# A hybrid attention block: VectorE's order written out in more places, results added to the output by stores, sums of weight chunks taken one chunk sooner in the last stage

## The chip, the core and the metric

The kernel runs on one core of one Trainium2 chip. The metric is the device time of one execution in microseconds. Three timed executions of the kernel before gave 2165.52, 2166.34 and 2167.77 us; the median is 2166.34. A profiled execution, taken separately, is where all durations come from.

## What is computed

One residual block over 512 tokens of width 2048, in float32:

```
h    = rms_norm(x) ; proj = h @ w_in          # 15424 columns, split into branches and gates
conv = (B * conv3(C * u)) * silu(conv_z) @ w_conv_out            # 1024 channels
mla  = attention(16 heads, low-rank q and kv, rotary keys, block-causal) * silu(mla_z) @ w_mla_out
memo = attention(4 heads of 256 over 256 memory tokens) * silu(mem_z) @ w_mem_out
merged = sigmoid(g1) * conv + sigmoid(g2) * mla + sigmoid(g3) * memo
out  = x + merged @ w_o
```

## The kernel before

**Products in three parts.** Each float32 operand is split into a high part, which ScalarE rounds to TensorE's reduced float32 (`act.activation(hi, src, Copy)`), and a low part, which VectorE subtracts (`lo = src - hi`). A product is three matmuls: high by high, high by low, low by high (`mm3`, L161 to L163). So every weight needs one ScalarE and one VectorE instruction before TensorE can use all of it.

**Panels.** The three large projections (w_h, the regrouped columns of w_in, then w_mla_out and w_o) use a scheme with seven products in place of eight for each 2x2 block of blocks. A panel is 256 output columns and takes four chunks of weights; per chunk TensorE makes 42 matmuls of 256 columns. `pair_weights` handles one chunk in three stages: load 512 KB into a `raw` tile (four buffers, L274); three VectorE sums of quarters into the same tile (L276 to L278); the split, `whi` by ScalarE (L281) and `wlo` by VectorE (L282), two buffers each. At a panel's end VectorE adds the four PSUM banks up into an `e` tile (L318 to L327, after a ScalarE copy at L317). The operand on the other side, `xp` or `xo`, is treated alike once for each of eight pairs: `pair_sums` (L255 to L258), then `pair_split` (L261, L262).

**The queue of chunks.** All weight chunks, of panels and of plain groups, stand in one list. `take` is called once for each chunk that TensorE is about to use: it brings this chunk and the next to the split, the one after to its sums, the fourth to its load, then runs one entry of `fills`, a list of postponed pieces of other work, and returns the chunk. Eight first chunks of a projection are ordered (0,0) (0,1) (0,2) (1,0) (1,1) (1,2) (0,3) (1,3) as (panel, chunk), so that pairs 6 and 7 of x can come late and two panels end one right after the other.

**Stages, in time.** Memory keys and values (four groups of eight chunks); x is normalised and split beside it; 60 w_h panels, whose results `finish` sends on (for the first eight panels the sums of squares and both parts, `keep_sums` and `keep_parts`); attention heads interleaved with their projections; the conv projection interleaved with memory attention (`mem_attend`, in the order `ORDER_MEM`: digits step a head, w steps the conv projection); w_mla_out; the memory projection in five groups, the last of four small chunks, beside which the merged results are loaded and turned into `xo`; w_o in eight panels, and the result. A step table, `steps_out`, says after which chunk of the memory projection each piece of merged work is done.

**Order on the engines.** TensorE's and SyncE's orders are those of the program text throughout. VectorE's is that of the text only inside a `manual_schedule` context: from step 27 of the memory keys to six steps into w_h, and from the memory projection to nine steps into w_o. Elsewhere a scheduler orders VectorE when the kernel is built, by its own estimate of times; it may also put an instruction from behind such a stretch between those of the stretch. ScalarE is always ordered by the scheduler. SyncE loads weights and most inputs; GpSimd issues loads and stores of scratch tensors, the accumulating stores into `mgdram` among them; ScalarE issues some stores.

**The result.** In each w_o panel but the last, `middle` (at the second chunk) loads the matching 512 KB of x into an `xr` tile (two buffers, L1341), and one chunk after the panel's end `result` adds `e` to it in two VectorE instructions (L1350) and stores the halves from ScalarE's queue (L1351). The last panel has a tail of its own, `tail_o`.

**Memory attention.** For each head two half steps of scores; each has a maximum (L1152), its scaled negative (L1155), two exponentials with their sums (L1159), a reciprocal (L1162) and two scalings of p (L1164). Then p is transposed by TensorE (L363), split, multiplied with the values, gated (L1180) and stored.

Of the kernel before, what the change touches and what calls it, by code (L numbers as in the profile page):

```python
# [20 lines left out]
F32 = mybir.dt.float32  # L21
# [86 lines left out]
def body(ctx, tc, a, out):  # L108
# [73 lines left out]

    def take(ahead=1):
        for at in range(1 + ahead):
            begin(at, 3)
        begin(1 + ahead, 2)
        begin(2 + ahead, 1)
        if fills:
            fills.pop(0)()
        return queue.pop(0)[4]  # L190
# [339 lines left out]
    work = panels(xp, a["w_h"], len(SEQUENCE), lambda n: make(n), lambda n, e: finish(n, e), "aux")  # L530
# [54 lines left out]
    begin(2, 2)  # L585
# [175 lines left out]

    def make(n):
        return etile(), None
# [57 lines left out]
    for _ in range(6):  # L821
        next(work)
# [15 lines left out]
    PLACES = ((2, 3), (6, 7), (4, 5), (0, 1))  # L838
# [292 lines left out]
    def mem_attend(head):  # L1131
# [11 lines left out]
        pr = []  # L1143
        for i2 in range(2):
# [16 lines left out]
            ri = pq.tile([P, 2], F32, tag="ri", name="ri", bufs=2)  # L1161
            vec.reciprocal(ri, sm)  # L1162
            for ii in range(2):
                act.activation(p[:, ii], p[:, ii], AF.Copy, scale=ri[:, ii:ii + 1])  # L1164
                pr.append(p[:, ii])
            yield
        pts = []
        for j in range(2):
            b = transpose4([t[:, j * P:(j + 1) * P] for t in pr])
# [19 lines left out]
    run(ORDER_MEM, w=conv, **{str(n): m[n] for n in range(4)})  # L1189
# [102 lines left out]
    def split_out(n):  # L1292
# [11 lines left out]
                 29: ((sums_out, 4),), 30: ((split_out, 4), (merged, 6)), 31: ((sums_out, 5),),  # L1304
                 32: ((split_out, 5),)}
# [9 lines left out]
    for tag, width in (("acc", 512), ("aux", 512), ("acc", 512), ("aux", 256), ("aux", 256)):  # L1315
        if done == 7:
            work = panels(xp, a["w_o"], 8, lambda n: make_o(n), lambda n, e: finish_o(n, e),
                          tail=lambda b, e: tail_o(b, e))
        banks = [bank(tag) for _ in range(width // P)]
# [18 lines left out]
    def make_o(n):  # L1338
        def middle():
            xrs[n] = pe.tile([P, 2, S], F32, tag="xr", name="xr", bufs=2)  # L1340
            nc.sync.dma_start(xrs[n].rearrange("p f n -> p (f n)"), a["xT"][:, n])  # L1341
        return pe.tile([P, 8, H], F32, tag="e", name="e", bufs=2), middle

    def finish_o(n, e):
        fills.append(lambda: result(n, e))

    def result(n, e):
        xr = xrs[n]
        for f in range(2):
            vec.tensor_tensor(out=xr[:, f], in0=two(e)[:, f], in1=xr[:, f], op=ALU.add)  # L1350
            nc.scalar.dma_start(out[(2 * n + f) * P:(2 * n + f + 1) * P], xr[:, f])  # L1351
# [16 lines left out]
    fills += [lambda: None, lambda: sums_out(6), lambda: split_out(6), lambda: sums_out(7), lambda: split_out(7)]  # L1368
# [82 lines left out]
```

## Time and profile before

| | us |
|---|---|
| median of three timed executions | 2166.34 |
| profiled execution, its own time | 2162.43 |
| span of its instructions | 2160.7 |
| TensorE busy | 2122.6 |
| VectorE busy | 1728.2 |
| ScalarE busy | 1010.8 |
| GpSimd busy | 130.9 |
| mean granted TensorE clock | 0.998 |

A line of a timeline has the start, the duration, the engine, the line of the program, the instruction, its output and inputs with shapes, and in brackets how long the engine sat idle before it and what ended that. A line of the view of waits has who waited for whom, the sum in us, how often, and the longest. Matmuls overlap, so their durations are longer than their spacing.

### The profile page before, as it was taken

How to read it: one execution, taken by the hardware profiler on the slowest of the kernel's cores; microseconds unless marked ns; L12 is line 12 of the kernel's file. 1: busy time of each engine (PE TensorE's matmuls, PEld its weight loads, DVE VectorE, ACT ScalarE, POOL GpSimd, SP SyncE). 2: the span in 40 equal slices, each digit the busy share in tenths (PEclk: the TensorE clock that was granted, in tenths of full speed). 3: DMA queues.
4: the chain of work that ended last, by engine and by line, in shares of the span. 5: the costliest groups of instructions: out<-in, count | busy, mean ns of one | idle time of the engine just before them, and what ended most of it. 6: DMA issues, size and time to landing. Idle time of an engine off the chain costs nothing.

```text
span 2160.7 us, 38707 instructions
## 1 busy us (share of the span) xinstructions
PE 2122.6 (98%) x16040; PEld 2037.7 (94%) x16040; DVE 1728.2 (80%) x2740; ACT 1010.8 (47%) x1235; POOL 130.9 (6%) x189
## 2 busy tenths in 40 slices
PE   9989999999999999999999999999999999999899
PEld 7889999999999999999999999898988899987899
DVE  5986878888888888888878876788886688856886
ACT  6743444444444344344444444777765533323333
POOL 0000000000000000000000000212111100011000
PEclk9999999999999999999999999999999999999999
DMA  8634443333333333343444336222346957667443
GB/s 330 248 98 137 158 135 128 128 127 128 127 127 127 125 125 126 126 136 133 137 137 142 131 129 241 90 104 81 112 158 245 355 203 208 201 213 199 141 162 107
DMA packets 93441, 338.51 MB, mean 157 GB/s; under 512 B 10896, under 2 KB 11152, under 8 KB 91216
## 3 DMA queue, kind: packets, MB, share of 16 engines
q1 hardware_dynamic: 70848, 252.58, 34.5%
q0 software_dynamic: 13920, 59.51, 8.6%
q10 hardware_dynamic: 8496, 23.94, 3.1%
q8 instruction: 125, 2.05, 0.4%
q14 instruction: 52, 0.43, 0.1%
HBM read 273.34 MB, written 62.65 MB: 156 GB/s over the span
## 4 chain that ended last, share of the span: by engine, by line
PE 84%; DVE 5%; ACT 2%; DMA 2%; issue 1%; POOL 0%; DVEq 0%; ACTq 0%; POOLq 0%
PE acc L161 14%; PE acc L163 14%; PE acc L162 14%; PE aux L161 13%; PE aux L163 13%; PE aux L162 13%; DVE wlo L282 2%; PE aux L363 1%; PE aux L997 1%; DMA raw<-in_w_h 1%; ACT whi L281 1%; DVE raw L276 0%; PE aux L977 0%; PE aux L980 0%; PE aux L978 0%
## 5 line engine op out<-in xcount | busy, mean ns | idle before, releaser
L281 ACT ACTIVATE whi<-raw 128x1792 fp32r<-128x1792 f32 x304 | 517.6, 1703 | 795.6 <-PE aux L162 336.7
L282 DVE TENSOR_TENSOR wlo<-raw,whi 128x1792 fp32r<-128x1792 f32 x304 | 614.8, 2022 | 204.2 <-ACT whi L281 203.5
L163 PE MATMUL aux<-xp,wlo 128*128 128x256 f32 (+1 forms) x1712 | 479.8, 280 | 6.3 <-DVE wlo L282 6.2
L161 PE MATMUL aux<-xp,whi 128*128 128x256 f32 (+1 forms) x1712 | 480.4, 281 | 0.0
L162 PE MATMUL aux<-xp,whi 128*128 128x256 f32 (+1 forms) x1712 | 479.2, 280 | 0.0
L163 PE MATMUL acc<-xp,wlo 128*128 128x256 f32 x1680 | 470.2, 280 | 3.4 <-DVE wlo L282 3.4
L161 PE MATMUL acc<-xp,whi 128*128 128x256 f32 x1680 | 470.8, 280 | 0.0
L162 PE MATMUL acc<-xp,whi 128*128 128x256 f32 x1680 | 469.6, 280 | 0.0
L163 PEld LDWEIGHTS aux<-xp,wlo 128*128 128x128 f32 (+1 forms) x1712 | 321.1, 188 | 7.5 <-DVE wlo L282 7.5
L161 PEld LDWEIGHTS aux<-xp,whi 128*128 128x128 f32 (+1 forms) x1712 | 320.6, 187 | 0.0
L163 PEld LDWEIGHTS acc<-xp,wlo 128*128 128x128 f32 x1680 | 316.0, 188 | 4.6 <-DVE wlo L282 4.6
L162 PEld LDWEIGHTS aux<-xp,whi 128*128 128x128 f32 (+1 forms) x1712 | 320.2, 187 | 0.0
L161 PEld LDWEIGHTS acc<-xp,whi 128*128 128x128 f32 x1680 | 315.6, 188 | 0.0
L162 PEld LDWEIGHTS acc<-xp,whi 128*128 128x128 f32 x1680 | 315.1, 188 | 0.0
L276 DVE TENSOR_TENSOR raw<-raw 128x512 f32<-128x512 f32 x304 | 208.3, 685 | 36.5 <-DMA raw<-in_w_h 31.8
L155 DVE TENSOR_TENSOR wlo<-raw,whi 128x1024 fp32r<-128x1024 f32 (+2 forms) x89 | 100.5, 1131 | 75.1 <-ACT whi L154 72.7
L154 ACT ACTIVATE whi<-raw 128x1024 fp32r<-128x1024 f32 (+2 forms) x89 | 87.7, 986 | 101.4 <-PE acc L162 43.3
L278 DVE TENSOR_TENSOR raw<-raw 128x256 f32<-128x256 f32 x304 | 127.9, 422 | 6.3
L277 DVE TENSOR_TENSOR raw<-raw 128x256 f32<-128x256 f32 x304 | 127.9, 422 | 5.7
L161 PE MATMUL acc<-whi,blk 128*128 128x384 f32 (+1 forms) x224 | 84.2, 376 | 0.0
L356 POOL TENSOR_TENSOR rs_r<-rs_t,mhalf 128x2 f32<-128x2 f32 (+2 forms) x71 | 65.2, 929 | 276.7 <-DVE rs_t L355 217.2
L163 PE MATMUL acc<-whi,blk 128*128 128x384 f32 (+1 forms) x224 | 80.9, 361 | 0.0
(360 smaller groups left out, 3896.7 us busy)
## 6 DMA issues: line engine op xcount, KB each, us to landing
raw<-in_w_h SPq DMA_DIRECT2D x240, 512.0 KB, 3.5
raw<-in_w_mla_out SPq DMA_DIRECT2D x32, 512.0 KB, 4.2
raw<-in_w_o SPq DMA_DIRECT2D x32, 512.0 KB, 3.6
raw<-in_w_mem_kv SPq DMA_DIRECT2D x31, 512.0 KB, 7.4
gdram<-e ACTq DMA_DIRECT2D x22, 512.0 KB, 2.9
raw<-in_w_ukv SPq DMA_DIRECT2D x16, 512.0 KB, 4.3
raw<-in_w_conv_out SPq DMA_DIRECT2D x16, 512.0 KB, 8.3
aadram<-z POOLq DMA_DIRECT2D x8, 896.0 KB, 3.9
```

The costliest lines, as they stand in the source:

```text
L154: act.activation(hi[:, cols], raw[:, cols], AF.Copy)
L155: vec.tensor_tensor(out=lo[:, cols], in0=raw[:, cols], in1=r32(hi[:, cols]), op=ALU.subtract)
L161: nc.tensor.matmul(o, lhsT=s[0], rhs=m[0], start=start, stop=False, skip_group_check=shared)
L162: nc.tensor.matmul(o, lhsT=s[0], rhs=m[1], start=False, stop=False, skip_group_check=shared)
L163: nc.tensor.matmul(o, lhsT=s[1], rhs=m[0], start=False, stop=stop, skip_group_check=shared)
L276: vec.tensor_tensor(out=f[:, 4:6], in0=f[:, 1:3], in1=f[:, 0:1].to_broadcast([P, 2, 256]), op=ALU.add)
L277: vec.tensor_tensor(out=f[:, 6], in0=f[:, 5], in1=f[:, 1], op=ALU.add)
L278: vec.tensor_tensor(out=f[:, 7], in0=f[:, 6], in1=f[:, 3], op=ALU.add)
L281: act.activation(hi, f[:, 1:8], AF.Copy)
L282: vec.tensor_tensor(out=lo, in0=f[:, 1:8], in1=r32(hi), op=ALU.subtract)
L356: pool.tensor_tensor(out=r, in0=t, in1=mhalf[:, :n], op=ALU.pow)
L363: nc.tensor.transpose(out=b[:, i * P:(i + 1) * P], in_=s, identity=ident)
```

## The change

Ten edits, in the order of the program:

- `take` gets a list `deeper`; for each entry in it the sums and the load reach one chunk further. An entry is put in ahead of the last group of the memory projection, so from there on sums are done for the third and fourth chunk, and the load for the fifth.
- `finish` of the first two w_h panels is postponed by way of `fills`.
- Ahead of w_h, its third chunk is only loaded (`begin(2, 1)`), not summed.
- In w_h panels 12 to 18, SyncE copies x, 512 KB a panel, from its input in DRAM straight to the output in DRAM.
- VectorE's written order in w_h ends after nine steps, not six.
- The places in memory of two pairs of latent blocks are exchanged (`PLACES`).
- In `mem_attend` the reciprocal and scalings of the first half step follow the exponentials of the second, and those of the second stand ahead of the first transposes.
- The run over `ORDER_MEM` gets a written VectorE order.
- The split of pair 5 of the merged results moves from the end of the memory projection to the first w_o chunk (to `fills`, where the empty entry was).
- The results of the first seven w_o panels are added to the output by accumulating stores from GpSimd's queue, straight from `e`, as soon as the panel's sums are done. Their x loads, additions and ScalarE stores go.

```diff
     def take(ahead=1):
         for at in range(1 + ahead):
             begin(at, 3)
-        begin(1 + ahead, 2)
-        begin(2 + ahead, 1)
+        more = 1 + ahead + len(deeper)
+        for at in range(1 + ahead, 1 + more):
+            begin(at, 2)
+        begin(1 + more, 1)
         if fills:
             fills.pop(0)()
         return queue.pop(0)[4]
...
-    work = panels(xp, a["w_h"], len(SEQUENCE), lambda n: make(n), lambda n, e: finish(n, e), "aux")
+    work = panels(xp, a["w_h"], len(SEQUENCE), lambda n: make(n),
+                  lambda n, e: fills.append(lambda: finish(n, e)) if n < 2 else finish(n, e), "aux")
...
-    begin(2, 2)
+    begin(2, 1)
...
+    def out_rows(n):
+        return out[2 * n * P:2 * (n + 1) * P].rearrange("(f p) n -> p f n", f=2)
+
     def make(n):
+        if n >= 12 and n < 19:
+            nc.sync.dma_start(out_rows(n - 12), a["xT"][:, n - 12].rearrange("p (f n) -> p f n", f=2))
         return etile(), None
...
-    for _ in range(6):
+    for _ in range(9):
         next(work)
     manual_dve.close()
...
-    PLACES = ((2, 3), (6, 7), (4, 5), (0, 1))
+    PLACES = ((2, 3), (4, 5), (6, 7), (0, 1))
...
+        def scaled(p, sm):
+            ri = pq.tile([P, 2], F32, tag="ri", name="ri", bufs=2)
+            vec.reciprocal(ri, sm)
+            for ii in range(2):
+                act.activation(p[:, ii], p[:, ii], AF.Copy, scale=ri[:, ii:ii + 1])
+                pr.append(p[:, ii])
+
+        waiting = []
...
-            ri = pq.tile([P, 2], F32, tag="ri", name="ri", bufs=2)
-            vec.reciprocal(ri, sm)
-            for ii in range(2):
-                act.activation(p[:, ii], p[:, ii], AF.Copy, scale=ri[:, ii:ii + 1])
-                pr.append(p[:, ii])
+            waiting.append((p, sm))
+            if i2 == 1:
+                scaled(*waiting[0])
             yield
         pts = []
         for j in range(2):
+            if j == 0:
+                scaled(*waiting[1])
...
-    run(ORDER_MEM, w=conv, **{str(n): m[n] for n in range(4)})
+    with tc.manual_schedule(engines={DVE}):
+        run(ORDER_MEM, w=conv, **{str(n): m[n] for n in range(4)})
...
-                 29: ((sums_out, 4),), 30: ((split_out, 4), (merged, 6)), 31: ((sums_out, 5),),
-                 32: ((split_out, 5),)}
+                 29: ((sums_out, 4),), 30: ((split_out, 4), (merged, 6)), 31: ((sums_out, 5),)}
...
+            deeper.append(1)
...
     def make_o(n):
         def middle():
-            xrs[n] = pe.tile([P, 2, S], F32, tag="xr", name="xr", bufs=2)
-            nc.sync.dma_start(xrs[n].rearrange("p f n -> p (f n)"), a["xT"][:, n])
+            if n == 7:
+                xrs[n] = pe.tile([P, 2, S], F32, tag="xr", name="xr", bufs=1)
+                nc.sync.dma_start(xrs[n].rearrange("p f n -> p (f n)"), a["xT"][:, n])
...
     def finish_o(n, e):
-        fills.append(lambda: result(n, e))
-
-    def result(n, e):
-        xr = xrs[n]
-        for f in range(2):
-            vec.tensor_tensor(out=xr[:, f], in0=two(e)[:, f], in1=xr[:, f], op=ALU.add)
-            nc.scalar.dma_start(out[(2 * n + f) * P:(2 * n + f + 1) * P], xr[:, f])
+        nc.gpsimd.dma_start(out_rows(n), two(e), accum_op=ALU.add)
...
-    fills += [lambda: None, lambda: sums_out(6), lambda: split_out(6), lambda: sums_out(7), lambda: split_out(7)]
+    fills += [lambda: split_out(5), lambda: sums_out(6), lambda: split_out(6), lambda: sums_out(7), lambda: split_out(7)]
```

More of the change, by code (lines that the diff above doesn't have):

```diff
@@ L181, in begin @@
                 entry.append(next(entry[1]))
+    deeper = []
     def take(ahead=1):
```

## The prediction

> **What bounds the kernel now.** I read the page first: how full is TensorE, and is a second engine near it?
>
> ```profile
> span 2160.7 us, 38707 instructions
> PE 2122.6 (98%) x16040; PEld 2037.7 (94%) x16040; DVE 1728.2 (80%) x2740; ACT 1010.8 (47%) x1235; POOL 130.9 (6%) x189
> L276 DVE TENSOR_TENSOR raw<-raw 128x512 f32<-128x512 f32 x304 | 208.3, 685 | 36.5 <-DMA raw<-in_w_h 31.8
> L278 DVE TENSOR_TENSOR raw<-raw 128x256 f32<-128x256 f32 x304 | 127.9, 422 | 6.3
> ```
>
> TensorE is busy 2122.6 of 2160.7 us. No matmul is removed by the change, so at most the 38.1 us of gaps can go, 1.8% of the time. The views of waits say what ends the gaps, and where (engine, line, what it waited for: us, times, longest). The two windows are the start of the w_h panels and the start of the w_o panels.
>
> ```profile
> PE acc L163 <- DVE wlo L282: 13.6, 12, 2.6
> PE aux L163 <- DVE wlo L282: 8.2, 10, 3.0
> PE aux L363 <- ACT p L1164: 2.4, 3, 1.7
> ...
> PE aux L163 <- DVE wlo L282: 5.4, 3, 3.0
> PE acc L163 <- DVE wlo L282: 3.4, 4, 1.4
> ...
> PE acc L163 <- DVE wlo L282: 9.8, 7, 2.6
> PE aux L163 <- DVE wlo L282: 1.0, 4, 0.2
> PE acc L161 <- ACT whi L281: 0.5, 1, 0.5
> ```
>
> The first three rows are the whole span, the next two 105 to 155 us, the last three 1975 to 2060 us. Nearly all of the loss on panel weights is in the two starts: 8.8 and 11.3 us. The third place is memory attention, 2.4 us. The change touches exactly these, so the limit at each is what I read next, in the timeline of VectorE.
>
> In steady panels the cadence is TensorE's:
>
> ```profile
> 395.82 2.02 DVE L282 TENSOR_TENSOR wlo<-raw,whi 128x1792 fp32r<-128x1792 f32 x1 [1.40 <-ACT whi L281]
> 400.77 2.03 DVE L282 TENSOR_TENSOR wlo<-raw,whi 128x1792 fp32r<-128x1792 f32 x1 [1.40 <-ACT whi L281]
> ```
>
> One chunk takes 4.95 us. VectorE spends 2.0 on its split and 0.69 + 2 x 0.42 = 1.5 on its sums. That leaves 1.4 for everything else, and the rest of its slack is idle waiting for ScalarE, which waits for TensorE. In the two starts VectorE has additional work (panels of x, merged results), so there TensorE follows VectorE's order.
>
> **Part 1, the start of w_h.**
>
> ```profile
> 105.04 2.03 DVE L282 TENSOR_TENSOR wlo<-raw,whi 128x1792 fp32r<-128x1792 f32 x1 [0.38 <-ACT whi L281]
> ...
> 110.44 0.69 DVE L276 TENSOR_TENSOR raw<-raw 128x512 f32<-128x512 f32 x1
> 111.96 2.02 DVE L282 TENSOR_TENSOR wlo<-raw,whi 128x1792 fp32r<-128x1792 f32 x1
> 115.08 1.23 DVE L497 TENSOR_TENSOR e<-e,xscale 128x1024 f32<-128x1024 f32 x1 [1.10 <-ACT e L496]
> ...
> 142.47 0.69 DVE L276 TENSOR_TENSOR raw<-raw 128x512 f32<-128x512 f32 x1 [3.01 <-DMA raw<-in_w_h]
> ...
> 143.54 2.02 DVE L282 TENSOR_TENSOR wlo<-raw,whi 128x1792 fp32r<-128x1792 f32 x1
> ...
> 149.13 0.69 DVE L276 TENSOR_TENSOR raw<-raw 128x512 f32<-128x512 f32 x1 [1.84 <-DMA raw<-in_w_h]
> ```
>
> Two faults show. The sums of the third chunk (110.44) stand ahead of the split of the second (111.96), though TensorE needs the split first: 1.5 us. And after the written order ends (six steps) the scheduler puts sums whose load has not landed ahead of a split that is due: VectorE idles 3.01 and 1.84 us.
>
> With the change the third chunk's sums follow the second split, and nine steps are written out. I lay VectorE's work out in the new order: split of the second chunk from 110.4, its end 112.4; then per chunk sums 1.5, one of the four pieces of x (1.2 + 1.5 or 2.0), split 2.0. Splits end at 112.4, 118.5, 124.0, 130.2, 135.6, 140.8, 146.0. TensorE, at 4.95 per chunk from 107.1 (the end of the first split) and with two matmuls possible before it needs the low part (0.24), waits 0.2, 0.9, 0.3, 1.0, 0.3, 0.1, 0.1. Then come two panel ends in succession, 2.3 us of sums of banks each (two at 0.69, three at 0.42, less overlap), and the two held-back finishes, each 1.4 us, now placed behind a split. The split of the tenth chunk then ends at 157.4 where 155.8 is due: 1.4. The sum is 4.3 us against 8.8, a gain of 4.5. Bounds: 0, if the scheduler again slips an early sum in, and 8.8.
>
> **Part 2, memory attention.** Again VectorE's order is the cause.
>
> ```profile
> 1653.17 1.22 DVE L155 TENSOR_TENSOR wlo<-raw,whi 128x1024 fp32r<-128x1024 f32 x1 [2.74 <-ACT whi L154]
> 1654.32 1.28 DVE L1152 TENSOR_REDUCE mx<-aux 128x2 f32<-128x512 f32 x2
> ...
> 160.00:180.00 20.00, 19.06 (x151) 18.98 (x150) 14.03 (x24) 8.59 (x8) 1.27 (x2) 0.91 0.51 184
> ...
> 1320.00:1340.00 20.00, 20.00 (x154) 19.27 (x154) 9.11 (x10) 7.77 (x10) 1.03 (x5) 1.00 0.92 336
> ...
> 1660.00:1680.00 20.00, 18.25 (x101) 15.53 (x101) 13.43 (x25) 14.98 (x38) 1.60 (x3) 0.91 0.47 171
> ```
>
> The lower rows are stretches of 20 us: busy time of PE, PEld, DVE, ACT and POOL, the granted clock, the DMA share, GB/s. The maxima of the first head (L1152) queue behind a split of conv weights that itself idles 2.74 us. The exponentials and scalings then pile up on ScalarE (15.0 of 20 us), and TensorE waits 1.7 us for the scaled p. In written order the maxima come first, 2.7 us sooner, which is more than the 1.7. The delayed reciprocals let ScalarE run the second exponentials before the first scaling and keep VectorE from standing on a sum. I take the 1.7 as gone (bounds 0 and 2.4). What is queued behind a waiting instruction now is the conv split; it has a chunk of lead, and VectorE works here for 13.4 of 20 us, so I cost the new waits at nothing; without that lead they cost up to the same 2.7.
>
> The granted clock is 0.91 in this stretch: 20 x 0.09 = 1.8 us lost. Yet longer waits, up to 2.6 us, after 1975 go with no dip. I count the 1.8 in, since the light stretch ahead of it goes (bounds 0 and 1.8); without it the sum below is 13.2. The Trainium skill ("TensorE: Matmul & The Clock Gate", Part 1: The HAM clock gate) says that the clock is halved after about one idle window of 3.4 us and comes back after a busy one; by it this dip goes with the wait. The trace agrees in part: one dip follows this wait, none follows those after 1975.
>
> **Part 3, the start of w_o.**
>
> ```profile
> 1983.17 0.39 PE L163 MATMUL aux<-am,wlo 128*128 128x512 f32 x1
> ...
> 1984.08 2.02 DVE L282 TENSOR_TENSOR wlo<-raw,whi 128x1792 fp32r<-128x1792 f32 x1 [0.38 <-ACT whi L281]
> ...
> 2026.85 0.68 DVE L318 TENSOR_TENSOR e<-acc,e 128x512 f32<-128x512 f32 x1
> ...
> 2028.96 0.69 DVE L276 TENSOR_TENSOR raw<-raw 128x512 f32<-128x512 f32 x1 [0.64 <-DMA raw<-in_w_o]
> ...
> 2030.57 2.01 DVE L282 TENSOR_TENSOR wlo<-raw,whi 128x1792 fp32r<-128x1792 f32 x1
> ...
> 2034.45 1.28 DVE L1350 TENSOR_TENSOR xr<-e,xr 128x512 f32<-128x512 f32 x2
> ...
> 2038.16 2.01 DVE L282 TENSOR_TENSOR wlo<-raw,whi 128x1792 fp32r<-128x1792 f32 x1
> ```
>
> Deeper taking moves each chunk's sums one chunk forward, two of them (3.0 us) into the last memory group, where VectorE idles. The first split gains little, since the sums of the next chunk take the freed place: it ends at 1985.8 instead of 1986.1, and TensorE, out of memory work at 1983.4, waits 1.8 us in all. From the second on, each split starts 1.5 to 2 us sooner and no longer waits for a high part that ScalarE could only make after late sums. Laid out as above (split, sums, one piece of merged work of 1.5 or 2.0, with the split of pair 5 behind the second split), splits end at 1985.8, 1990.8, 1996.3, 2001.3, 2006.8, 2011.8, 2017.3, 2020.8, 2027.2, 2033.3; waits are 1.8, 0, 0, 0, 0.4, 0, 0.3, 0, 0, 0.8, in all 3.3 against 11.3. The removed additions (1.28 a panel; 2034.45 stands ahead of the split that TensorE then waited 2.6 us for) are in this. Gain 8.0; bounds 0 and 11.3.
>
> The loads themselves don't start sooner after the fourth chunk: there are four raw buffers, and a load goes out when the split four chunks before ends.
>
> ```profile
> 2038.03 0.33 SPq L1341 DMA_DIRECT2D xr<-in_xT  x1
> 2038.46 0.38 SPq L274 DMA_DIRECT2D raw<-in_w_o  x1
> 2040.20 0.33 SPq L274 DMA_DIRECT2D raw<-in_w_o  x1
> ```
>
> 2040.20 is the end of the split at 2038.16. The load at 2038.46 stood behind xr on SP's queue, which waited for its buffer; that xr goes, and with it this block.
>
> **Part 4, the copies and stores.**
>
> ```profile
> raw<-in_w_h SPq DMA_DIRECT2D x61, 512.0 KB, 3.5
> ...
> mgdram<-sg POOLq DMA_DIRECT2D x6, 512.0 KB, 5.6
> ...
> DMA to landing us min/median/max: 5.3/7.0/12.1
> ...
> DVE raw L276 <- DMA raw<-in_w_h: 26.5, 18, 3.6
> ```
>
> An accumulating store like the new ones lands in 5.6 us while mla_out's panels run (the third row is that of the later mgdram stores). It holds an e buffer wanted two panels, 39.6 us, later, and on POOL nothing but the next store queues behind it: nothing. The last such store has a panel less its sums, 19.8 - 2.3 = 17.5 us, to the end. The copy of x to the output, seven times in the w_h panels, is in no row; it moves as much as a load and writes HBM too, so 3.5 to 12.1 us. It goes on SP right behind one load and 4.95 ahead of the next, and the trace forgave lateness: 18 sums waited for loads between 170 and 1315 us, the longest 3.6, and of the span's 21.8 us of waits for a low part the two starts have 8.8 and 10.8, so that 2.2 are left for all other panels. I take 1 us in all; bounds 0 and, at 12.1 each, 7 x (12.1 - 4.95 - 3.6) = 25. The nearest row is the plain load, hence the low end. The order of the blocks meets a TensorE that is full from 1320 to 1340; nothing, and the latent loads' delay beyond that cover if a block falls on a buffer freed late.
>
> **Sum.** 4.5 + 1.7 + 1.8 + 8.0 - 1.0 = 15.0 us. The profiled execution took 2162.43 (span 2160.7) and would take 2147.4; the runs' median is 2166.34, 3.9 above it, and the gain is taken off that: 2151.3.
>
> **Rivals.** *One start gives nothing*: the scheduler, free after nine steps, again slips sums ahead of a due split, as at 142.47 and 2028.96; for this speaks that nothing in the change forbids it, against that the splits concerned are then past the double panel end. Losing the larger gain leaves 7.0: 2159.3. *A second dip goes*: another, 0.91 again, lies in 160 to 180 us; if a TensorE that no longer starves before it isn't throttled there, 1.8 more: 2149.5. Against it, the light stretch there is that of the tiny matmuls of the sums, and they stay. *The waits only trade places*: strict order makes VectorE stand on bank sums and maxima as long as it stood on loads; 13.4 of the 15.0 return: 2164.7. *Slower*: the copies hold the rings in front of weight loads; the whole gain is used up, and 0.2% (4.3 us, about what can be told from no change) more, when each copy costs (15.0 + 1.0 + 4.3) / 7 = 2.9 us of TensorE, that is from 4.95 + 3.6 + 2.9 = 11.5 us per copy on, which only the longest stores reach; at 12.1 the time is 2166.3 - 16.0 + 25 = 2175.3. The Trainium skill ("DMA: Bandwidth & Descriptors", Issuing engines are not separate DMA queues) says that transfers of all queues share the same 16 engines, which speaks for this rival.
>
> **Numbers.** Forecast 0.50, one start 0.25, second dip 0.10, trade 0.08, slower 0.07. Faster by over 0.2%: 0.85; within: 0.08; slower: 0.07. The low end takes parts 1 to 3 near, though not all at, their upper bounds (20.3 us): 2146.0. The high end reaches past the lost start to a gain of 3.8: 2162.5. Outside lie the last two cases and little else.
>
> **What would show it.** Right: panel waits near 4 us in 105 to 155 and near 3 after 1975, no wait of 1.7 for p, clock 1.0 there, no L1350 pairs before the last panel. Wrong: sums waiting for loads ahead of splits behind the ninth chunk; new TensorE waits at the seven copies (12 panels of 19.8 behind the start, from about 350 to 475 us), which would mean slower.

## The result, and the profile after

The changed kernel takes 2173.49 us (median of seven executions, 2171.11 to 2177.59), the kernel before, run beside it, 2165.52 (2163.70 to 2167.77). The ratio is 1.0044 with a 95% interval of 1.0033 to 1.0055: slower by 0.4%, where 2151.3 us, 15.0 less than before, was forecast. The profiled execution took 2171.11, against 2162.43 before. Lines of the changed program stand a few numbers further on: raw sums L281 to L283, `whi` L286, `wlo` L287, the memory heads' maxima L1174, exponentials L1181, reciprocals L1160, scalings L1162, transposes L368, the accumulating store L1370.

The page's first lines, then the view of waits over the whole span (us, times, longest):

```profile
span 2169.2 us, 38662 instructions
...
PE 2128.2 (98%) x16040; PEld 2045.2 (94%) x16040; DVE 1720.4 (79%) x2726; ACT 1012.6 (47%) x1235; POOL 138.9 (6%) x196
```

```profile
PE acc L163 <- DVE wlo L287: 12.1, 8, 4.8
PE aux L368 <- ACT p L1162: 10.3, 3, 4.0
PE aux L163 <- DVE wlo L287: 6.9, 6, 3.1
```

VectorE did lose work (1720 for 1728 us), and the waits for panel weights fell from 21.8 to 19.0 us. But the wait for the scaled p of memory attention, which was to vanish, went from 2.4 to 10.3. For each stage I take the time from its first matmul to the next stage's first (from w_h to the latents: to the last matmul of w_h), from the timeline of TensorE:

| stage, us | before | after | difference |
|---|---|---|---|
| w_h panels | 1228.96 | 1228.23 | -0.7 |
| latents, heads | 310.87 | 311.00 | +0.1 |
| memory attention with conv | 89.04 | 100.20 | +11.2 |
| w_mla_out | 160.12 | 162.48 | +2.4 |
| memory projection | 88.45 | 87.07 | -1.4 |
| w_o, to the start of its last matmul | 171.86 | 168.88 | -3.0 |

The sum, 8.6, is the span's growth of 8.5 us but for what lies ahead of w_h and behind the last matmul. The loss lies in memory attention and just behind it; the two panel stages gained 3.7 of the 12.5 forecast for their starts.

**Memory attention.** Stretches of 20 us (busy time of PE, PEld, DVE, ACT and POOL, clock, DMA share, GB/s):

```profile
1640.00:1660.00 20.00, 18.53 (x112) 16.29 (x110) 11.01 (x23) 10.23 (x27) 2.64 (x5) 1.00 0.60 221
1660.00:1680.00 20.00, 15.08 (x66) 12.28 (x67) 9.96 (x19) 8.93 (x19) 1.05 (x2) 0.74 0.26 101
1680.00:1700.00 20.00, 16.00 (x83) 13.37 (x82) 10.29 (x22) 12.38 (x31) 2.34 (x6) 0.91 0.56 190
```

No engine is full: TensorE falls to 15.1 of 20 us, VectorE and ScalarE to half, so they wait for each other. The timelines of VectorE, ScalarE and TensorE show the circle:

```profile
1648.01 0.68 DVE L1174 TENSOR_REDUCE mx<-aux 128x2 f32<-128x512 f32 x1
...
1653.32 0.17 DVE L1160 RECIPROCAL ri<-sm 128x2 f32<-128x2 f32 x1 [3.64 <-ACT p L1181]
...
1657.78 1.29 DVE L132 TENSOR_TENSOR mv<-mvr,mv 128x512 fp32r<-128x512 f32 x2 [1.16 <-ACT mv L130]
1659.39 0.23 DVE L1160 RECIPROCAL ri<-sm 128x2 f32<-128x2 f32 x2 [0.32 <-ACT p L1181]
```

```profile
1651.13 1.06 ACT L154 ACTIVATE whi<-raw 128x1024 fp32r<-128x1024 f32 x1 [2.11 <-PE acc L162]
1652.10 0.55 ACT L1181 ACTIVATE p<-aux,nm,mqs 128x256 f32<-128x256 f32 x1
...
1659.59 0.57 ACT L1181 ACTIVATE p<-aux,nm,mqs 128x256 f32<-128x256 f32 x1 [0.23 <-DVE ri L1160]
...
1660.69 1.69 ACT L1162 ACTIVATE p<-p,ri 128x256 f32<-128x256 f32 x4
```

```profile
1662.04 1.73 PE L368 MATMUL aux<-ident,p 128*128 128x128 f32 x6 [3.50 <-ACT p L1162]
...
1669.57 1.16 PE L368 MATMUL aux<-ident,p 128*128 128x128 f32 x6 [2.82 <-ACT p L1162]
...
1691.24 1.09 PE L368 MATMUL aux<-ident,p 128*128 128x128 f32 x3 [4.00 <-ACT p L1162]
```

The maxima are early, as forecast: 1648.01 against 1654.32. ScalarE, in its scheduler's order, follows only in part. As before, the high part of conv weights stands ahead of the exponentials and waits 2.11 us for TensorE; the exponentials start at 1652.10 (1656.18 before), though their input is there by 1649.7. VectorE stands 3.64 us on their sums with everything written behind them. What is left of the lead is lost at the first head's second half step. Its exponentials are done at 1656.4, but its reciprocal is written behind the second head's maxima, a split of the values and the second head's first reciprocal: it is the second of the two at 1659.39. ScalarE then runs the second head's last exponentials and, of the four scalings in a row from 1660.69, the second head's two first. TensorE, which had transposed the first half step's p at 1658.15, goes on at 1662.04, as the third of them ends, after 3.50 us; the kernel before waits 1.68 there. Beside these waits of 2.8 to 4.0 us TensorE's clock is low as well: 0.74 and 0.91.

**The start of w_h.** TensorE's two long waits, then VectorE's order ahead of them:

```profile
153.29 0.39 PE L163 MATMUL aux<-xp,wlo 128*128 128x256 f32 x1 [1.89 <-DVE wlo L287]
...
161.62 0.38 PE L163 MATMUL aux<-xp,wlo 128*128 128x256 f32 x1 [3.11 <-DVE wlo L287]
```

```profile
149.62 0.69 DVE L281 TENSOR_TENSOR raw<-raw 128x512 f32<-128x512 f32 x1 [0.56 <-DMA raw<-in_w_h]
...
151.22 2.02 DVE L287 TENSOR_TENSOR wlo<-raw,whi 128x1792 fp32r<-128x1792 f32 x1
...
157.02 0.68 DVE L281 TENSOR_TENSOR raw<-raw 128x512 f32<-128x512 f32 x1
...
159.55 2.02 DVE L287 TENSOR_TENSOR wlo<-raw,whi 128x1792 fp32r<-128x1792 f32 x1
```

Through the eighth chunk the splits end as laid out. Behind that sums stand again ahead of due splits, now beside the double panel end, and the ninth and tenth chunk wait. All waits of this start are 8.5 us (8.8 before).

**The start of w_o.** TensorE, VectorE, SyncE's queue and GpSimd, each from its timeline:

```profile
2048.70 0.58 PE L163 MATMUL acc<-xo,wlo 128*128 128x256 f32 x1 [4.82 <-DVE wlo L287]
```

```profile
2045.02 0.69 DVE L281 TENSOR_TENSOR raw<-raw 128x512 f32<-128x512 f32 x1 [3.61 <-DMA raw<-in_w_o]
...
2046.63 2.01 DVE L287 TENSOR_TENSOR wlo<-raw,whi 128x1792 fp32r<-128x1792 f32 x1
```

```profile
2038.53 0.33 SPq L279 DMA_DIRECT2D raw<-in_w_o  x1
```

```profile
2036.87 1.22 POOL L1370 DMA_DIRECT2D out<-e  x1 [28.85 <-DVE e L332]
```

The first nine splits ended as laid out (the stage starts 11.2 us later than before), the ninth at 2038.5, and the waits up to there were 1.9 us. Then the scheduler put the thirteenth chunk's sums, whose load had been issued at 2038.53 and took 6.5 us beside the first accumulating store, ahead of the split that was due: VectorE idle for 3.61 us, TensorE for 4.82.

**The copies.** The stretch of six of them, before and after, and their DMA row (KB each, median us to landing):

```profile
360.00:480.00 120.00, 120.00 (x1022) 120.00 (x1021) 100.10 (x137) 49.82 (x38) 1.06 (x2) 1.00 0.39 131
```

```profile
360.00:480.00 120.00, 120.00 (x1021) 120.00 (x1020) 100.64 (x137) 49.30 (x38) 1.06 (x2) 1.00 0.47 156
```

```profile
out<-in_xT SPq DMA_DIRECT2D x7, 512.0 KB, 5.1
```

TensorE is full in both. The copies cost nothing there.

### The profile page after: what moved, and what is told of

The parts are those of the page before. It is cut to its first block, busy times and chain, and to the rows that moved or that the text cites. A ratio compares the mean times of both kernels' runs of the same rounds, so it can differ in the third digit from the quotient of the medians.

```text
span 2169.2 us, 38662 instructions
## 1 busy us (share of the span) xinstructions
PE 2128.2 (98%) x16040; PEld 2045.2 (94%) x16040; DVE 1720.4 (79%) x2726; ACT 1012.6 (47%) x1235; POOL 138.9 (6%) x196
## 4 chain that ended last, share of the span: by engine, by line
PE 90%; DVE 5%; ACT 2%; issue 2%; DMA 1%; SPq 0%; POOL 0%; DVEq 0%; ACTq 0%; POOLq 0%
PE acc L163 16%; PE acc L162 16%; PE acc L161 15%; PE aux L163 13%; PE aux L162 13%; PE aux L161 13%; DVE wlo L287 2%; PE aux L1010 1%; PE aux L368 1%; DVE raw L281 0%; PE aux L990 0%; PE acc L648 0%; ACT whi L286 0%; PE aux L993 0%; PE aux L991 0%
## 5 line engine op out<-in xcount | busy, mean ns | idle before, releaser
L286 ACT ACTIVATE whi<-raw 128x1792 fp32r<-128x1792 f32 x304 | 517.7, 1703 | 785.6 <-PE aux L162 358.0
L287 DVE TENSOR_TENSOR wlo<-raw,whi 128x1792 fp32r<-128x1792 f32 x304 | 614.6, 2022 | 201.4 <-ACT whi L286 200.2
L281 DVE TENSOR_TENSOR raw<-raw 128x512 f32<-128x512 f32 x304 | 208.0, 684 | 40.8 <-DMA raw<-in_w_h 26.0
L283 DVE TENSOR_TENSOR raw<-raw 128x256 f32<-128x256 f32 x304 | 128.0, 421 | 6.6
```

What stands on the lines that cost most here:

```text
L281: vec.tensor_tensor(out=f[:, 4:6], in0=f[:, 1:3], in1=f[:, 0:1].to_broadcast([P, 2, 256]), op=ALU.add)
L283: vec.tensor_tensor(out=f[:, 7], in0=f[:, 6], in1=f[:, 3], op=ALU.add)
L286: act.activation(hi, f[:, 1:8], AF.Copy)
L287: vec.tensor_tensor(out=lo, in0=f[:, 1:8], in1=r32(hi), op=ALU.subtract)
```

## The experiments

All start from the changed kernel. Ratios are to the kernel before, run beside each, with their 95% intervals. "Old memory attention" below means the first experiment's edit.

### Memory attention

My theory was that both edits here do harm; its rival, that the loss comes from the clock or from elsewhere and shows there only. First, both undone:

```diff
-    with tc.manual_schedule(engines={DVE}):
-        run(ORDER_MEM, w=conv, **{str(n): m[n] for n in range(4)})
+    run(ORDER_MEM, w=conv, **{str(n): m[n] for n in range(4)})
...
-            waiting.append((p, sm))
-            if i2 == 1:
-                scaled(*waiting[0])
+            scaled(p, sm)
...
-            if j == 0:
-                scaled(*waiting[1])
```

> The changed kernel with memory attention as it was before (no written VectorE order there, scalings right behind their exponentials); all else of the change stays. Theory A: the time was lost in memory attention, where TensorE's stage grew from 89.0 to 100.2 us in the profiles, with 10.3 us of waits for p in place of 2.4 and three stretches of halved clock. Then this kernel takes about 11 to 13 us less than the changed one, 2160 to 2163, and the stage is near 89 again. Theory B: the copies of x and the accumulating stores slow the weight loads all along. Then most of the loss stays and the time is 2168 or more.

Measured: 2159.14 us, 0.9975 (0.9964 to 0.9986). Memory attention takes 88.66 us, w_mla_out 160.22. Its waits for p and the stretch that had the low clock:

```profile
PE aux L368 <- ACT p L1162: 3.3, 4, 1.7
```

```profile
1660.00:1680.00 20.00, 17.04 (x97) 13.95 (x96) 13.05 (x26) 16.38 (x41) 1.07 (x2) 1.00 0.53 187
```

The two edits cost 1.0044 - 0.9975 = 0.7%, some 15 us (each ratio is uncertain by 0.0011, so give or take 3), of which the traces show 11.5 in the stage and 2.3 behind it. The rest of the change is a gain. In this trace the 1.7 us wait stands and the clock is 1.00: the wait doesn't always bring the dip (the last section shows why).

Next, each edit alone: the written order with the old scaling, and the late scaling with the scheduler's order.

```diff
-            waiting.append((p, sm))
-            if i2 == 1:
-                scaled(*waiting[0])
+            scaled(p, sm)
...
-            if j == 0:
-                scaled(*waiting[1])
```

> The changed kernel with the scalings of p back at their old place, but with the written VectorE order in memory attention. Theory A1: the written order is what costs, since VectorE stands on ScalarE's exponentials and all else queues behind. Then it is as slow as the changed kernel, 2170 to 2175. Theory A2: the late scaling costs, since the second reciprocal stands behind the other head's work. Then it is near the kernel with memory attention as before, 2158 to 2163, and the waits for p are under 2.4 us.

```diff
-    with tc.manual_schedule(engines={DVE}):
-        run(ORDER_MEM, w=conv, **{str(n): m[n] for n in range(4)})
+    run(ORDER_MEM, w=conv, **{str(n): m[n] for n in range(4)})
```

> The changed kernel without the written order in memory attention, but with the late scalings. Theory A1 (the order costs): near the kernel with memory attention as before, 2160 to 2163. Theory A2 (the late scaling costs): 2168 or more, waits for p of 8 us or more.

Measured: the order alone 2172.54, 1.0042 (1.0029 to 1.0056), memory attention 96.56 and w_mla_out 168.38; the late scaling alone 2163.48, 1.0000 (0.9989 to 1.0011), memory attention 93.66. The first is as the order's theory said, the second just above its 2160 to 2163. Against 0.9975 the order costs 0.7% and the late scaling 0.25%. Together they cost no more than the order alone, so the two prices don't add. Waits of the first, in memory attention and from 1725 to 1800 us, and TensorE's longest of the second:

```profile
PE aux L368 <- ACT p L1162: 6.6, 5, 1.8
...
PE acc L163 <- DVE wlo L287: 3.5, 2, 1.9
PE aux L163 <- DVE wlo L287: 2.3, 1, 2.3
```

```profile
1663.39 1.73 PE L368 MATMUL aux<-ident,p 128*128 128x128 f32 x6 [3.57 <-ACT p L1162]
```

In written order each wait for p is short, but there are more, and VectorE comes late to w_mla_out: 5.8 us of waits there, 1.3 with the old memory attention. The timelines of VectorE show where that comes from, first with both edits undone, then with the order alone:

```profile
1724.93 0.69 DVE L281 TENSOR_TENSOR raw<-raw 128x512 f32<-128x512 f32 x1
...
1736.76 0.68 DVE L281 TENSOR_TENSOR raw<-raw 128x512 f32<-128x512 f32 x1
```

These are the first sums of w_mla_out. The scheduler puts them among the conv splits, 11.7 us ahead of that stage's first matmul; in the run with the written order they come behind the last conv split, 6.3 us ahead, after VectorE has idled 3.46 us for that split's high part. The first weight split of the stage ends 1.66 us ahead of its first matmul in the one, and 1.95 us behind it in the other. The figures 6.3 and 1.95 are the same in the changed kernel, which loses 2.4 us there. No run moves these sums by themselves.

The late scaling brings one long wait by itself. With both edits undone TensorE's transposes at the same place are

```profile
1660.93 0.73 PE L368 MATMUL aux<-ident,p 128*128 128x128 f32 x2 [0.18 <-ACT p L1162]
...
1663.34 1.17 PE L368 MATMUL aux<-ident,p 128*128 128x128 f32 x6 [1.68 <-ACT p L1162]
```

Both transpose the first half step's p 13 us into the stage. The second half step's p, scaled late, comes 1.9 us later, so that TensorE waits 3.57 us for it in place of 1.68; the stage's waits for p are 6.9 us in place of 3.3, and a dip of the clock of 6.83 us lies beside the longest.

Does the harm of the order lie in where the scalings stand, or in VectorE's standing on ScalarE at all? Both scalings went to the end of the second half step, and then ScalarE was put into the written order too.

```diff
             if i2 == 1:
                 scaled(*waiting[0])
+                scaled(*waiting[1])
...
-            if j == 0:
-                scaled(*waiting[1])
```

> The changed kernel with its written order in memory attention, but the scalings of both half steps right behind the exponentials of the second, ahead of the other head's work. Theory F: written order and late scaling each put something ahead of a reciprocal that TensorE waits for; with both reciprocals here VectorE stands only once per head on ScalarE, and the stage takes 88 to 91 us in place of 100.2: 2158 to 2163. Rival: VectorE standing on ScalarE at all, with conv splits behind it, is the loss; then the stage is 95 us or more and the time over 2167.

```diff
-    with tc.manual_schedule(engines={DVE}):
+    with tc.manual_schedule(engines={DVE, ACT}):
```

> Both scalings of p stand at the end of a head's second half step, and in memory attention VectorE's and ScalarE's orders are both the written one; all else as in the changed kernel. With both scalings there but ScalarE scheduled, memory attention took 95.6 us (88.7 with the old code) and TensorE waited 3.1 and 3.8 us for the scaled p. Theory: the loss comes of a written VectorE against a ScalarE whose scheduler puts the conv high parts ahead of the exponentials; with both written alike the exponentials follow the maxima at once, and memory attention takes 89 us or less, waits for p under 2 us in all, time 2158 to 2161. Rival: it is the written interleaving itself (the step order puts conv steps between) that makes each engine stand on the others; then ScalarE in written order stands on TensorE's scores as well, and the stage takes 94 us or more, time 2166 or over.

Measured: 2166.80, 1.0015 (1.0005 to 1.0026), memory attention 95.64, w_mla_out 161.0; then 2168.27, 1.0014 (1.0001 to 1.0026), 91.37 and 165.16. Waits of the second from 1645 to 1790 us (its lines stand one further on):

```profile
PE acc L164 <- DVE wlo L288: 3.5, 2, 1.9
PE aux L164 <- DVE wlo L288: 1.9, 1, 1.9
PE aux L162 <- ACT p L1182: 1.8, 1, 1.8
PE aux L369 <- ACT p L1163: 1.2, 1, 1.2
```

Moving the scalings cures a part: 1.0044 to 1.0015 is some 6 of the 15 us (uncertain by 3). The stage is the rival's, the time just below it. With ScalarE written out as well the waits on ScalarE's p, scaled or not, fall from 6.9 to 3.0 us, so an order written for one engine against a scheduler's on its partner is part of the loss. But 5.4 us of waits for low parts come up at w_mla_out (1.9 in the run before). The first sums of that stage stand 6.3 us ahead of it here too, and 8.7 in the run before. Nothing is gained in all. Neither theory of the last run came out: its stage lies between the two forecasts, its time is the rival's.

### The last stage

Is the deeper taking at fault for the 4.82 us? With the old memory attention:

```diff
-            deeper.append(1)
```

> The changed kernel with memory attention as before and without the deeper taking. Theory C: deeper taking is what makes the one long wait of the w_o panels, 4.8 us at the tenth chunk, because the scheduler puts sums of the 13th chunk ahead of the tenth's split and their load can't start before the ninth's split frees its buffer; with it goes the halved clock of 6.8 us behind it. Then it is 4 to 7 us faster than the kernel with memory attention as before, 2154 to 2158. Rival: earlier sums are worth what part 3 of the prediction gave them; then it is 2 to 4 us slower than that kernel, 2163 to 2167.

Measured: 2165.59, 1.0010 (1.0002 to 1.0019); w_o 173.29 against 167.99. The theory falls: without deeper taking the ratio is 0.0035 higher (7.6 us, uncertain by 3) and w_o 5.3 us longer, so it pays, though it is the sums so moved that the scheduler misplaces. Then the output path, again with the old memory attention (the old x loads, additions and stores; no copies):

```diff
-        nc.gpsimd.dma_start(out_rows(n), two(e), accum_op=ALU.add)
+        fills.append(lambda: result(n, e))
```

> The changed kernel with memory attention as before and with the output written as before: x loaded, added by VectorE and stored in each w_o panel, no copies ahead, no accumulating stores. Theory D: the stores are a gain, since 1.3 us of VectorE's work a panel and the xr loads on SyncE's queue go; then this kernel is 2 to 5 us slower than the one with the new output (2159.1), 2161 to 2164, and w_o takes 170 to 173 us in place of 168.0. Rival: the accumulating stores slow the weight load that the tenth split's wait hangs on (6.5 us to landing beside a store, 3.8 elsewhere), and the copies slow the w_h panels; then it is 2 to 4 us faster, 2155 to 2157.

Measured: 2155.31, 0.9968 (0.9954 to 0.9981), w_o 164.80. The new path saves nothing here: 0.9968 and 0.9975 can't be told apart, and in the traces w_o is 3.2 us shorter without it. The scheduler puts the thirteenth chunk's sums ahead of the due split in this run too, but their load landed 3.4 us after its issue (VectorE, then TensorE):

```profile
2030.20 0.69 DVE L281 TENSOR_TENSOR raw<-raw 128x512 f32<-128x512 f32 x1 [0.17 <-DMA raw<-in_w_o]
...
2034.81 0.39 PE L163 MATMUL acc<-xo,wlo 128*128 128x256 f32 x1 [2.37 <-DVE wlo L287]
```

VectorE idles 0.17 us for it in place of 3.61, and TensorE waits 2.37 in place of 4.82 (4.36 with the old memory attention and the new path). To see what the wait is when those sums stay behind the split, the written order goes on for six more steps, with the new path:

```diff
-        if n == 8:
+        if n == 14:
             manual_dve.close()
```

> The changed kernel with memory attention as before, VectorE's written order kept for 15 steps of w_o in place of nine. Theory E: the long wait at the tenth chunk (4.8 us) comes from sums that the scheduler moved there from behind the written part; with more steps written they can't come so far ahead, the wait is under 1.5 us, the halved clock behind it goes, and w_o takes 162 to 165 us in place of 168.0: 2153 to 2156. Rival: VectorE has simply too much work at the double panel end; then the wait stays at 4 us and the time within 2 us of 2159.

Measured: 2154.16, 0.9956 (0.9943 to 0.9970), w_o 163.83. The waits from 1975 to 2060 us are

```profile
PE acc L163 <- DVE wlo L287: 2.5, 2, 1.9
```

where the changed kernel has 6.7. The thirteenth load, beside the first store, takes 6.3 us here as well, but its sums now stand behind the split, and the tenth chunk waits 0.6 us. So the wait goes with the misplaced sums, as the theory said; how long it was, the slow load had a part in. Both together, the old path and 15 written steps:

```diff
-        nc.gpsimd.dma_start(out_rows(n), two(e), accum_op=ALU.add)
+        fills.append(lambda: result(n, e))
...
-        if n == 8:
+        if n == 14:
```

> Memory attention as before, the result by the old path (x loads, VectorE additions, ScalarE stores; no copies, no accumulating stores), and VectorE's order written through 15 steps of w_o in place of 9. The new path with 15 written steps gave 2154.2 and a w_o of 163.8 us; the old path with 9 steps 2155.3 and 164.8. Theory: the new path's one harm in w_o was the hoisted sums waiting for a slow load beside the first store; written through, both paths are alike, since the additions removed (1.28 us a panel) lie in VectorE's slack: w_o 163 to 164.5, time 2153 to 2155. Rival: stores beside loads, and copies in w_h, cost something in every panel; then the old path is shorter by over 2 us: w_o under 162.5, time under 2152.

Measured: 2153.44, 0.9952 (0.9939 to 0.9965), w_o 165.91. By the times the two paths are alike; the w_o of this one trace is longer than either forecast. This and the run before it are faster than both kernels, and not to be told apart.

### The start of w_h

The same cure, with the old memory attention:

```diff
-    for _ in range(9):
+    for _ in range(15):
         next(work)
```

> The changed kernel with memory attention as before, VectorE's written order kept for 15 steps of w_h in place of nine. Theory E: of the waits of 1.9 and 3.1 us at the ninth and the eleventh chunk most goes, w_h takes 3 to 5 us less than 1229, 2154 to 2157. Rival: VectorE is full there (two panel ends, two finishes); then the waits move to later chunks and the time stays within 2 us of 2159.

Measured: 2160.02, 0.9969 (0.9953 to 0.9986); w_h 1231.34. The 1.89 and 3.11 us (at the ninth and tenth chunk) are gone, and others stand in their place:

```profile
161.14 0.39 PE L163 MATMUL aux<-xp,wlo 128*128 128x256 f32 x1 [2.09 <-DVE wlo L287]
...
188.71 0.38 PE L163 MATMUL acc<-xp,wlo 128*128 128x256 f32 x1 [2.41 <-DVE wlo L287]
```

At the first VectorE itself is behind, without any idle time from 147.7 to 163.9; ahead of the second it stood 4.31 us on ScalarE's high part. VectorE's order alone doesn't mend this, as the rival said. So what are the w_h edits worth? They were taken out of the run with 15 written steps of w_o:

```diff
-                  lambda n, e: fills.append(lambda: finish(n, e)) if n < 2 else finish(n, e), "aux")
+                  lambda n, e: finish(n, e), "aux")
...
-    begin(2, 1)
+    begin(2, 2)
...
-    for _ in range(9):
+    for _ in range(6):
```

> Memory attention as before and 15 written steps of w_o (2154.2 us, w_h 1227.2 us), and the start of w_h as in the kernel before: third chunk's sums ahead of w_h, no finish postponed, six written steps. Theory: the edits at w_h only moved its waits from the first eight chunks to the ninth and tenth; w_h is as long as before, 1228 to 1230 us, and the time 2154 to 2157. Rival: the sooner first seven splits are a gain of some 4 us, as forecast at 4.5, and hidden in the traces by the dips of the clock; without them w_h takes 1231 us or more and the time is 2158 or over.

Measured: 2162.51, 0.9997 (0.9987 to 1.0006), by its figures the rival's. But 7.5 us of it are in another stage, the latent projections, 318.36 us for 310.9, where TensorE waits for the latent blocks and SyncE's queue for a buffer (waits of TensorE, then of SyncE's queue):

```profile
PE acc L161 <- DMA blk<-latdram: 4.6, 2, 3.8
```

```profile
SPq L862 <- DMA gdram<-e: 19.8, 1, 19.8
```

So the exchange of places got undone as well:

```diff
-    PLACES = ((2, 3), (4, 5), (6, 7), (0, 1))
+    PLACES = ((2, 3), (6, 7), (4, 5), (0, 1))
```

> As the run with w_h as before and 15 written steps of w_o (2162.5 us; w_h 1232.9, the latent projections 318.4 where all other kernels have 310.9), but the places of the latent blocks are also those of the kernel before. Theory: the exchange of places belongs to the postponed finishes, which shift by one the rotation of the buffers that the blocks' memory was made of; with the old finishes and the new places the third pair of block loads stood 19.8 us on SyncE's queue behind a store from such a buffer, against 8.8 with both old and 9.0 with both new. With both old the projections take 310.9 again, and the start of w_h, as before, loses nothing against the changed one: time 2154 to 2156.5. Rival: the w_h edits are worth the forecast 4.5 us; then w_h takes 1231 us or more and the time is 2158 or over.

Measured: 2157.55, 0.9965 (0.9952 to 0.9979); projections 310.95, w_h 1228.38, and the wait of the queue is 9.6 us. The theory of the places holds in so far as tried: both old (8.8 and 9.6 us on the queue) and both new (9.2) are alike, old finishes with new places cost 7.5 us. The fourth pairing, new finishes with the old places, was not run. As for the w_h edits, the time lies a little above one forecast and under the other, w_h in the theory's. Last, the edits that seemed to pay, alone: before, with deeper taking, the split of pair 5 moved, and 15 written steps. Shown against the kernel before, without the lines of `take` that use `deeper`, which are those of the change:

```diff
+            deeper.append(1)
...
-                 32: ((split_out, 5),)}
...
-    fills += [lambda: None, lambda: sums_out(6),
+    fills += [lambda: split_out(5), lambda: sums_out(6),
...
-        if n == 8:
+        if n == 14:
```

> The kernel before with three edits alone: chunks taken one deeper from the last memory group on, the split of pair 5 in the first w_o chunk, and VectorE's order written through 15 steps of w_o. Old w_h start, old places, old memory attention, results by the old path. Theory: these three are all of the change that pays; with the old path and the changed w_h start the time was 2153.4, so 2152 to 2155.5. Rival: the w_h start is worth the forecast 4.5 us and was hidden by the clock's dips in single traces: 2157 or over.

Measured: 2156.70, 0.9959 (0.9944 to 0.9974). Against the same kernels with the new w_h start (0.9956 and 0.9952) these two runs are 0.0009 and 0.0007 slower, 1.9 and 1.5 us. Each ratio is uncertain by 0.0013 to 0.0015, so the mean of both, 1.7 us, is uncertain by about 3: between nothing and the forecast 4.5.

## Why the prediction was wrong

**Part 2 failed, and with it the sign.** The step reads "In written order the maxima come first, 2.7 us sooner, which is more than the 1.7", and "I cost the new waits at nothing". The maxima came 6 us sooner, and the first exponentials 4. But I laid out VectorE alone, and only to the first wait. ScalarE's order, which the change doesn't touch, kept a high part of conv weights ahead of the exponentials; VectorE stood on them, and the reciprocal that TensorE's next transposes hang on stood behind the other head's work. Waits for p went from 2.4 to 10.3 us. Behind the stage the first sums of w_mla_out came 5.4 us later against its start. The forecast gain of 3.5 became a loss of some 15 by the runs against the kernel with both edits undone, of which the clock is a part: 1.00, 0.91 and 1.00 over three stretches before became 1.00, 0.74 and 0.91. The bounds, "0 and 2.4", left out a loss altogether, although the text had seen that VectorE's waits have something queued behind them. And "The delayed reciprocals let ScalarE run the second exponentials before the first scaling" was taken for a gain; alone it cost 5 us, since the second half step's p reached TensorE 1.9 us later. The 1.8 for the clock hung on chance: with both edits undone the 1.7 us wait stands, and no dip follows.

**Part 3 was right in its cause and missed one step.** The splits up to the ninth came as laid out, and the waits with them: 1.9 us where 2.5 were forecast, 1.8 of these at the first chunk. The tenth was counted at 0.8 and took 4.82. I had let the order run past its written nine steps as if it were written; in "One start gives nothing" the scheduler does just this, and I held against it that the splits concerned are past the double panel end. They were beside it, and the sums waited for a load that the new stores slow, 6.5 us to landing, where Part 4 had counted the stores at nothing. With the order written to 15 steps the waits are 2.5, less than the 3.3 forecast, and w_o is 8.0 us shorter than before (171.86 to 163.83), the forecast term to the tenth. That is partly luck, since a dip of the clock took 1.8 us of the gain back. The additions counted in it were worth nothing: the old path does as well.

**Part 1** had its first seven splits right and missed the sums ahead of splits behind them: 8.5 us of waits for 4.3. Its lower bound, "0, if the scheduler again slips an early sum in", is what came.

**Part 4** was right that copies hold up nothing in steady panels, and its 1.0 us for them should have been 0: 5.1 us each, none of it on TensorE. Its stores are harmless in steady panels, not at the start of w_o. The order of blocks did cost nothing, for the reason given as its condition: no block on a buffer freed late; the experiment without the postponed finishes shows that price, 7.5 us.

**The rivals.** "The waits only trade places" came near the mechanism, VectorE standing still in its strict order; but it stood on ScalarE's exponentials, not on bank sums and maxima. It was priced as if the waits could at most return, by 13.4 us for which no working is given, and they grew. "Slower" was sought in the copies, which were innocent. The sum: 15.0 us of gain forecast, 8.7 of loss in the profiled execution. Of the 23.7 between them, memory attention and the start of w_mla_out make 17.0 (3.5 forecast, 13.5 lost), w_h 3.8, w_o 5.0, less 1.0 for the copies and 1.4 in the memory projection.

## What to carry to other kernels

An order written out for one engine is only as good as the orders of the engines that feed it: lay out all partners of a chain, here VectorE, ScalarE and TensorE, before calling a wait gone, and give a written wait a price above nothing when work stands behind it. Writing the partner out too is not enough: here it cut the waits for p, and the next stage's first sums still came too late. So look at what the written stretch keeps out as well. Where a written order ends, the scheduler may put work that waits on a transfer ahead of work that is due; carry the order on past the point at which buffers and panel ends coincide, and look at the first chunk behind it. Edits that turn a buffer's rotation have partners elsewhere in the program, so undo them together or the experiment measures the mismatch.

## What the runs showed of the hardware

The clock's dip is not fixed by the length of the wait before it. Two runs have the same program from memory attention to the end (15 written steps of w_o, the new and the old w_h start), and each waits once for a low part at the start of w_o, 1.87 us in the one with the new w_h start and 2.18 in the one with the old. From 1980 to 2000 us the clock is 0.91 in the first and 1.00 in the second: the shorter wait has the dip. Cut into steps of 3.41 us the traces show why (first run, then second; PE's busy time stands behind the length, the clock third from the end):

```profile
1982.43:1985.84 3.41, 1.54 (x11) 1.26 (x10) 3.34 (x5) 2.99 (x2) 0.00 (x0) 1.00 0.56 227
1985.84:1989.25 3.41, 3.41 (x18) 3.41 (x18) 3.38 (x5) 0.31 (x1) 0.87 (x1) 0.50 0.49 156
```

```profile
1980.80:1984.21 3.41, 2.40 (x12) 1.81 (x10) 3.27 (x7) 2.00 (x2) 0.00 (x0) 1.00 0.77 229
1984.21:1987.62 3.41, 2.25 (x19) 2.25 (x20) 3.34 (x6) 1.90 (x2) 0.00 (x0) 1.00 0.54 185
1987.62:1991.03 3.41, 3.41 (x32) 3.41 (x31) 3.37 (x4) 0.71 (x1) 0.87 (x1) 1.00 0.56 88
```

The steps are taken from the dips. In the changed kernel's trace dips last 3.41 or 6.83 us and start at 162.09, 172.33, 1660.54, 1670.78, 1691.26, 1998.46 and 2046.25 us, all whole multiples of 3.413 us apart; other traces have the same steps, shifted. The whole wait of the first run lies in one step, which leaves 1.54 us of work in it, and the next step has half the clock. In the second run a step ends at 1984.21, in the middle of the wait, and each side keeps over 2.2 us of work. So too the 1.68 us wait of memory attention: in the kernel before it lies whole in the step that ends at 1663.31, where the dip starts; with both edits undone a step ends in the middle of it, at 1662.18. From 110 to 2140 us of all fifteen traces, thirty steps at full clock had more than 1.9 us without a matmul, and each was followed by a dip; of 39 with 1.2 to 1.8 us, among ordinary matmuls (no transposes, no tiny matmuls of the sums), one was.

The Trainium skill ("TensorE: Matmul & The Clock Gate", Part 1: The HAM clock gate) says that the window over which activity is judged runs freely and doesn't start with the kernel, so that the outcome varies with the phase; these rows agree. It also speaks of one idle window of about 3.4 us, and here 1.87 us of waiting was enough. It follows that one trace's stage can be some 2 us longer than another's with the same program in that stage (20 x 0.09 = 1.8), and that a dip behind a wait of 2 us can't be put into a forecast as certain, as I did with 1.8 us, since where the steps will lie is not known beforehand.

An accumulating store of 512 KB lands in 6.2 us (median of seven) and a copy of 512 KB from DRAM to DRAM in 5.1, against 3.8 for a load of w_o. A load beside such a store is slower: in the changed kernel six loads of w_o were issued within 3 us behind one and took 5.5 to 6.5 us; of the loads from the thirteenth on, the eleven with no such store in flight took 3.4 to 4.6. In the eleven traces with these stores the medians are 5.8 us (66 loads) and 3.5 (105); in the three with the old path it is 3.6 (60).
